# The first loads of an instance norm, split by even and odd partitions over two DMA queues

## The chip, the cores and the metric

The kernel runs on one core of one Trainium2 chip. The metric is the device time of one execution in microseconds (us), as the median of several runs.

## The reference

The input x has the shape 4 x 8 x 16 x 256 x 256 in float32 (134 MB). Each of its 4 x 8 x 16 = 512 channels, of 256 x 256 elements, is normalised by its own mean and variance and multiplied by a gamma per channel.

```python
def reference(x, gamma):
    mu = x.mean(axis=(3, 4), keepdims=True)
    var = ((x - mu) ** 2).mean(axis=(3, 4), keepdims=True)
    x_norm = (x - mu) / np.sqrt(var + 1e-5)
    out = x_norm * gamma[None, :, :, None, None]
    return out.astype(np.float32)
```

## The kernel before

The 512 channels are taken in 32 units of 16 channels. A channel is spread over 8 partitions, so a unit is one tile of 128 partitions x 8192 elements, 4 MiB, that lies in one piece in memory. Six such tiles, `slots`, hold the units in turn: unit u lies in `slots[u % 6]`.

The schedule is written out by hand, so each engine takes its instructions in the order of the code. Before the loop, two small transfers go out on the GpSimd queue: `touch` (8 KB, line 54) and the gamma row `g_row` (line 55). Then units 0 to 5 are loaded (line 48): units 1 and 3 on ScalarE's DMA queue, units 0, 2, 4 and 5 on SyncE's. GpSimd makes the averaging matrix `navg`, and VectorE (DVE) and TensorE (PE) spread gamma over the partitions: `g_rep` (line 81), `g_ps` (line 86) and `g_col` (line 92). These stand ahead of unit 0's work on DVE.

The loop then takes the units one by one. DVE sums the tile (line 105) while ScalarE (ACT) sums its squares (line 106). PE multiplies both sums with `navg` (line 114), which gives minus the mean and minus the mean square of each channel on all of its partitions. DVE, ACT and DVE turn these into the scale (lines 115, 119, 123, 125), and DVE applies mean and scale to the tile in place (line 128). The tile is stored on ScalarE's queue (line 132), and SyncE's queue loads unit u + 6 into the same slot, once that store has landed.

A transfer that is issued waits in its queue for those ahead of it; the two queues are served beside one another. The wait for a semaphore is done by the engine that issues (SyncE or ScalarE) and holds up what that engine would issue next.

Of the kernel before, what the change touches and what calls it, by code (L numbers as in the profile page):

```python
# [1 line left out]

# [4 lines left out]

F32 = mybir.dt.float32
U8 = mybir.dt.uint8
ALU = mybir.AluOpType  # L10
ACTF = mybir.ActivationFunctionType
AX = mybir.AxisListType


@with_exitstack
def kernel(
    ctx: ExitStack,
    tc: tile.TileContext,
    x: bass.AP,
    gamma: bass.AP,  # L20
    out: bass.AP,
):
    nc = tc.nc
    B, G, C, H, W = x.shape
    P = nc.NUM_PARTITIONS
    HW = H * W
    n_ch = B * G * C
    S = 8
    K = P // S
    F = HW // S  # L30
    U = n_ch // K
    NG = (G * C) // K
    AHEAD = 6
    assert HW % S == 0 and (G * C) % K == 0

    xv = x.rearrange("b g c h w -> (b g c h w)").rearrange("(u p f) -> u p f", p=P, f=F)
    ov = out.rearrange("b g c h w -> (b g c h w)").rearrange("(u p f) -> u p f", p=P, f=F)
    gv = gamma.rearrange("g c -> (g c)")

    data = ctx.enter_context(tc.tile_pool(name="data", bufs=1))  # L40
    singles = ctx.enter_context(tc.tile_pool(name="singles", bufs=1))
    psum = ctx.enter_context(tc.tile_pool(name="psum", bufs=4, space=bass.MemoryType.PSUM))
    ctx.enter_context(tc.manual_schedule())

    slots = [data.tile([P, F], F32, name=f"xt{i}") for i in range(AHEAD)]

    def load(u, queue):
        queue.dma_start(out=slots[u % AHEAD][:], in_=xv[u])  # L48


    g_row = singles.tile([1, G * C], F32, name="g_row")
    touch = singles.tile([16, 128], F32, name="touch")
    nc.vector.memset(touch[:], 0.0)  # L53
    nc.gpsimd.dma_start(out=ov[0][0::S, 0:128], in_=touch[:])  # L54
    nc.gpsimd.dma_start(out=g_row[:], in_=gv[None, :])  # L55
    for u in range(AHEAD):
        load(u, nc.scalar if u in (1, 3) else nc.sync)


    eps_t = singles.tile([P, 1], F32, name="eps_t")  # L60
    nc.gpsimd.memset(eps_t[:], 1e-5)
    one = singles.tile([1, 1], F32, name="one")
    nc.gpsimd.memset(one[:], 1.0)
    navg = singles.tile([P, K, S], F32, name="navg")
    nc.gpsimd.memset(navg[:], -1.0 / HW)  # L65
    nc.gpsimd.affine_select(  # L66
        out=navg[:], in_=navg[:], pattern=[[-S, K], [0, S]], compare_op=ALU.is_ge,
        fill=0.0, base=0, channel_multiplier=1,
    )
    nc.gpsimd.affine_select(  # L70
        out=navg[:], in_=navg[:], pattern=[[S, K], [0, S]], compare_op=ALU.is_ge,
        fill=0.0, base=S - 1, channel_multiplier=-1,
    )
    navg_w = navg[:].rearrange("p k s -> p (k s)")
    root_eps = singles.tile([P, 1], F32, name="root_eps")
    nc.scalar.activation(out=root_eps[:], in_=eps_t[:], func=ACTF.Sqrt)  # L76
    g_rep = singles.tile([1, NG, K, S], F32, name="g_rep")
    g_ps = psum.tile([P, NG], F32, name="g_ps", bufs=1)
    g_col = singles.tile([P, NG], F32, name="g_col")

    nc.vector.tensor_copy(  # L81
        out=g_rep[:],
        in_=g_row[:].rearrange("o (n k) -> o n k", n=NG).unsqueeze(3).to_broadcast([1, NG, K, S]),
    )
    for n in range(NG):
        nc.tensor.matmul(  # L86
            out=g_ps[:, n : n + 1],
            lhsT=g_rep[:, n].rearrange("o k s -> o (k s)"),
            rhs=one[:],
            start=True, stop=True,  # L90
        )
    nc.vector.tensor_copy(out=g_col[:], in_=g_ps[:])  # L92

    junk = singles.tile([P, F], U8, name="junk")

    st = singles.tile([P, U, 2], F32, name="st")
    nvar = singles.tile([P, U], F32, name="nvar")
    std = singles.tile([P, U], F32, name="std")
    rstd = singles.tile([P, U], F32, name="rstd")
    scale = singles.tile([P, U], F32, name="scale")  # L100

    squares = []
    for u in range(U):
        t = slots[u % AHEAD]
        nc.vector.reduce_sum(out=st[:, u, 0:1], in_=t[:], axis=AX.X)  # L105
        square = nc.scalar.activation(  # L106
            out=junk[:], in_=t[:], func=ACTF.Square, accum_out=st[:, u, 1:2],
        )
        if u:

            tc.declare_no_dep(square.ins, squares[-1].ins, reason="junk, ordered by the root between")
        squares.append(square)
        ps = psum.tile([P, 2], F32, name="ps")
        nc.tensor.matmul(out=ps[:], lhsT=navg_w, rhs=st[:, u], start=True, stop=True)  # L114
        nc.vector.tensor_scalar(  # L115
            out=nvar[:, u : u + 1], in0=ps[:, 0:1], scalar1=ps[:, 0:1],
            scalar2=ps[:, 1:2], op0=ALU.mult, op1=ALU.add,
        )
        nc.scalar.activation(  # L119
            out=std[:, u : u + 1], in_=nvar[:, u : u + 1], func=ACTF.Sqrt,  # L120
            bias=eps_t[:], scale=-1.0,
        )
        nc.vector.reciprocal(out=rstd[:, u : u + 1], in_=std[:, u : u + 1])  # L123
        g = u % NG
        nc.vector.tensor_mul(  # L125
            out=scale[:, u : u + 1], in0=rstd[:, u : u + 1], in1=g_col[:, g : g + 1],
        )
        nc.vector.tensor_scalar(  # L128
            out=t[:], in0=t[:], scalar1=ps[:, 0:1], scalar2=scale[:, u : u + 1],
            op0=ALU.add, op1=ALU.mult,  # L130
        )
        nc.scalar.dma_start(out=ov[u], in_=t[:])
        if u + AHEAD < U:
            load(u + AHEAD, nc.sync)


# [1 line left out]
_INS = ['x', 'gamma']  # L138
_OUTS = [((4, 8, 16, 256, 256), 'float32')]


# [23 lines left out]
```

## Time and profile before

| what | value |
|---|---|
| median of 3 runs | 626.87 us (626.68 to 627.37) |
| profiled execution, span from first to last instruction | 625.4 us (the page lists no other time of this execution) |
| DVE busy | 443.4 us (71%) |
| ACT busy | 238.8 us (38%) |
| PE busy | 21.4 us (3%) |
| moved by DMA | 268.46 MB, mean 429 GB/s |
| loads, issue to landing, median | 38.5 us on SyncE's queue, 31.7 us on ScalarE's |
| stores, issue to landing, median | 62.5 us |
| first reduction of unit 0 (line 105) starts | 22.57 us |
| first store issued | 37.63 us |
| last load issued and landed | 547.2 us, 585.7 us |
| last store issued | 600.8 us |

The page and the trace show one execution. Times of instructions count from the first one. A group's line gives its busy time and the mean time of one instruction, then the idle time of the engine before it and what ended that. The queue q1 is SyncE's, q10 is ScalarE's and q0 is GpSimd's. A window's last two columns are the mean busy share of the 16 DMA engines and what they moved in GB/s; a transfer's packets can put that share slightly over 1.

### The profile page before, as it was taken

What the parts mean: (1) busy time and instruction counts of PE and PEld (TensorE: products, weight loads), DVE (VectorE), ACT (ScalarE), POOL (GpSimd) and SP (SyncE); (2) the same over time, 40 slices, a digit from 0 to 9 for tenths busy, and PEclk for the clock granted to TensorE, in tenths of its full rate; (3) what the DMA queues carried; (4) which work ended last, traced back from release to release, by engine and by line L of the source; (5) the groups of instructions that cost most, each with busy time, mean ns of one, the idle gap of its engine ahead of it and who ended that gap; (6) DMA issues with size and microseconds to landing.
All of it is one profiled execution on the core that took longest, in us unless ns stands there. A gap on an engine that the chain in (4) does not pass through costs nothing.

```text
span 625.4 us, 631 instructions
## 1 busy us (share of the span) xinstructions
PE 21.4 (3%) x80; PEld 19.5 (3%) x80; DVE 443.4 (71%) x163; ACT 238.8 (38%) x98; POOL 2.4 (0%) x11
## 2 busy tenths in 40 slices
PE   0200000000000000000000000000000000000000
PEld 0200000000000000000000000000000000000000
DVE  0588999999776687666776767867668676686730
ACT  0444444444443244432344423444224442244400
POOL 1000000000000000000000000000000000000000
DMA  8999999999999999999999999999999999999998
GB/s 369 436 402 436 436 436 436 436 434 424 434 436 432 432 428 434 436 436 436 436 434 423 434 436 432 436 428 434 434 436 436 436 436 432 425 434 434 434 432 363
DMA packets 9282, 268.46 MB, mean 429 GB/s; under 512 B 1072, under 2 KB 1088, under 8 KB 1088
## 3 DMA queue, kind: packets, MB, share of 16 engines
q10 hardware_dynamic: 4896, 142.61, 52.9%
q1 hardware_dynamic: 4320, 125.83, 46.7%
q0 software_dynamic: 64, 0.01, 0.0%
q14 instruction: 2, 0.02, 0.0%
HBM read 134.22 MB, written 134.23 MB: 429 GB/s over the span
## 4 chain that ended last, share of the span: by engine, by line
another core or an unknown queue 61%; DMA 17%; DVE 15%; SPq 1%; PE 1%; issue 0%; ACT 0%
DVE st L105 10%; DMA xt<-in_x_dram 10%; DMA out_dram<-xt 8%; DVE xt L128 5%; SPq L48 1%; PE ps L114 1%; ACT std L119 0%; DVE nvar L115 0%; DVE rstd L123 0%; DVE scale L125 0%
## 5 line engine op out<-in xcount | busy, mean ns | idle before, releaser
L105 DVE TENSOR_REDUCE st<-xt 128x1 f32<-128x8192 f32 x32 | 277.9, 8685 | 100.8 <-DMA xt<-in_x_dram 100.8
L106 ACT ACTIVATE junk<-xt 128x8192 uint8<-128x8192 f32 x32 | 225.0, 7030 | 275.6 <-DMA xt<-in_x_dram 232.4
L128 DVE TENSOR_SCALAR xt<-xt,ps,scale 128x8192 f32<-128x8192 f32 x32 | 145.6, 4551 | 1.2
L119 ACT ACTIVATE std<-nvar,eps_t 128x1 f32<-128x1 f32 x32 | 9.4, 295 | 79.6 <-DVE nvar L115 79.6
L114 PE MATMUL ps<-st,navg 128*128 128x2 f32 x64 | 17.8, 348 | 557.6 <-DVE st L105 557.6
L114 PEld LDWEIGHTS ps<-st,navg 128*128 128x128 f32 x64 | 16.0, 311 | 559.4 <-issue 559.4
L115 DVE TENSOR_SCALAR nvar<-ps 128x1 f32<-128x1 f32 x32 | 9.2, 288 | 23.8 <-PE ps L114 23.8
L123 DVE RECIPROCAL rstd<-std 128x1 f32<-128x1 f32 x32 | 5.3, 164 | 11.6 <-ACT std L119 11.6
L81 DVE COPY g_rep<-g_row 1x1024 f32<-1x1024 f32 x1 | 0.7, 681 | 14.2 <-DMA g_row<-in_gamma_dram 14.2
L106 ACT ACTIVATION_READ_ACCUMULATOR junk<-xt 128x1 f32 x32 | 6.0, 187 | 0.0
L125 DVE TENSOR_TENSOR scale<-rstd,g_col 128x1 f32<-128x1 f32 x32 | 5.1, 160 | 1.1
L86 PE MATMUL g_ps<-one,g_rep 1*128 1x1 f32 x16 | 3.5, 347 | 16.1 <-DVE g_rep L81 16.1
L86 PEld LDWEIGHTS g_ps<-one,g_rep 1*128 1x128 f32 x16 | 3.5, 326 | 16.1 <-issue 16.1
L92 DVE COPY g_col<-g_ps 128x8 f32<-128x8 f32 x1 | 0.2, 167 | 3.7 <-PE g_ps L86 3.7
L76 ACT ACT_TABLE_LOAD x1 | 1.3, 1283 | 1.7 <-PEq L149 1.7
L53 DVE MEMSET touch<- 16x128 f32 x1 | 0.2, 165 | 0.9 <-PEq L149 0.9
L54 POOL DMA_DIRECT2D out_dram<-touch x1 | 0.6, 617 | 0.8 <-DVE touch L53 0.8
L55 POOL DMA_DIRECT2D g_row<-in_gamma_dram x1 | 0.5, 484 | 0.0
L66 POOL TENSOR_SCALAR_AFFINE_SELECT navg<-navg 128x128 f32<-128x128 f32 x1 | 0.4, 398 | 0.1
L70 POOL TENSOR_SCALAR_AFFINE_SELECT navg<-navg 128x128 f32<-128x128 f32 x1 | 0.4, 397 | 0.1
L65 POOL MEMSET navg<- 128x128 f32 x1 | 0.2, 231 | 0.0
L76 ACT ACTIVATE root_eps<-eps_t 128x1 f32<-128x1 f32 x1 | 0.2, 203 | 0.0
(6 smaller groups left out, 0.6 us busy)
## 6 DMA issues: line engine op xcount, KB each, us to landing
out_dram<-xt ACTq DMA_DIRECT2D x32, 4096.0 KB, 62.5
xt<-in_x_dram SPq DMA_DIRECT2D x30, 4096.0 KB, 38.5
xt<-in_x_dram ACTq DMA_DIRECT2D x2, 4096.0 KB, 31.7
out_dram<-touch POOLq DMA_DIRECT2D x1, 8.0 KB, 9.1
g_row<-in_gamma_dram POOLq DMA_DIRECT2D x1, 0.5 KB, 13.3
```

The lines of the kernel that those rows point to most:

```text
L48: queue.dma_start(out=slots[u % AHEAD][:], in_=xv[u])
L76: nc.scalar.activation(out=root_eps[:], in_=eps_t[:], func=ACTF.Sqrt)
L81: nc.vector.tensor_copy(out=g_rep[:], in_=g_row[:].rearrange("o (n k) -> o n k", n=NG).unsqueeze(3).to_broadcast([1, NG, K, S]),)
L86: nc.tensor.matmul(out=g_ps[:, n : n + 1], lhsT=g_rep[:, n].rearrange("o k s -> o (k s)"), rhs=one[:], start=True, stop=True,)
L105: nc.vector.reduce_sum(out=st[:, u, 0:1], in_=t[:], axis=AX.X)
L106: square = nc.scalar.activation(out=junk[:], in_=t[:], func=ACTF.Square, accum_out=st[:, u, 1:2],)
L114: nc.tensor.matmul(out=ps[:], lhsT=navg_w, rhs=st[:, u], start=True, stop=True)
L115: nc.vector.tensor_scalar(out=nvar[:, u : u + 1], in0=ps[:, 0:1], scalar1=ps[:, 0:1], scalar2=ps[:, 1:2], op0=ALU.mult, op1=ALU.add,)
L119: nc.scalar.activation(out=std[:, u : u + 1], in_=nvar[:, u : u + 1], func=ACTF.Sqrt, bias=eps_t[:], scale=-1.0,)
L123: nc.vector.reciprocal(out=rstd[:, u : u + 1], in_=std[:, u : u + 1])
L125: nc.vector.tensor_mul(out=scale[:, u : u + 1], in0=rstd[:, u : u + 1], in1=g_col[:, g : g + 1],)
L128: nc.vector.tensor_scalar(out=t[:], in0=t[:], scalar1=ps[:, 0:1], scalar2=scale[:, u : u + 1], op0=ALU.add, op1=ALU.mult,)
```

## The change

Units 0 to 3 are loaded one after the other, each in two halves: SyncE's queue loads the even partitions (64 partitions with a step of 2), ScalarE's the odd ones. Unit 0 is stored in the same two halves, on both queues. The loads of units 4 and 5 are moved from ahead of the loop to behind unit 0's store, on SyncE's queue. All other stores and loads stay as they were.

```diff
     def load(u, queue):
         queue.dma_start(out=slots[u % AHEAD][:], in_=xv[u])
 
+    SHARED = 4
+
+    def halves(u):
+        return [(queue, slots[u % AHEAD][h::2, :], xs) for queue, h, xs in
+                ((nc.sync, 0, slice(0, P, 2)), (nc.scalar, 1, slice(1, P, 2)))]
+
...
-    for u in range(AHEAD):
-        load(u, nc.scalar if u in (1, 3) else nc.sync)
+    for u in range(SHARED):
+        for queue, rows, xs in halves(u):
+            queue.dma_start(out=rows, in_=xv[u][xs])
...
-        nc.scalar.dma_start(out=ov[u], in_=t[:])
+        if u == 0:
+            for queue, rows, xs in halves(u):
+                queue.dma_start(out=ov[u][xs], in_=rows)
+            for v in range(SHARED, AHEAD):
+                load(v, nc.sync)
+        else:
+            nc.scalar.dma_start(out=ov[u], in_=t[:])
         if u + AHEAD < U:
             load(u + AHEAD, nc.sync)
```

In the changed kernel SyncE's order is thus: four half loads, half of store 0, loads 4 and 5, then load 6 and on. ScalarE's is: four half loads, its work on unit 0, half of store 0, its work on unit 1, store 1, and on.

## The prediction

> **What bounds the kernel now.** I read the DMA part of the page first, because the kernel reads 134 MB and writes 134 MB and computes little.
>
> ```profile
> DMA packets 9282, 268.46 MB, mean 429 GB/s; under 512 B 1072, under 2 KB 1088, under 8 KB 1088
> ## 3 DMA queue, kind: packets, MB, share of 16 engines
> q10 hardware_dynamic: 4896, 142.61, 52.9%
> q1 hardware_dynamic: 4320, 125.83, 46.7%
> ```
>
> The two hardware queues' packets take 52.9 + 46.7 = 99.6% of what 16 DMA engines have in the span of 625.4 us. That is 622.9 us of transfer and 2.5 us in which an engine waits, start and last receipt included. No compute engine comes near: DVE is busy 443.4 us. The chain of waits says the same, in repeated steps:
>
> ```profile
> 179.79 18.95 another core or an unknown queue
> 198.74 0.02 SPq L48
> 198.77 0.03 issue
> 198.80 0.33 SPq L48
> 199.12 18.97 another core or an unknown queue
> ```
>
> One turn is 198.77 - 179.43 = 19.35 us, in which one unit is loaded and one stored: 9.67 us for a transfer of 128 x 8192. 64 of them are 619 us. The windows view, last two columns DMA share and GB/s, shows that no part of the run is left open:
>
> ```profile
> 20.00:40.00 20.00, 0.56 (x2) 0.50 (x2) 16.25 (x6) 9.39 (x4) 0.00 (x0) 1.00 0.98 421
> 40.00:60.00 20.00, 0.56 (x2) 0.50 (x2) 18.82 (x6) 12.48 (x5) 0.00 (x0) 1.00 1.01 418
> 100.00:560.00 460.00, 13.94 (x50) 12.53 (x50) 341.15 (x125) 183.19 (x75) 0.00 (x0) 1.00 1.00 433
> 600.00:620.00 20.00, 0.00 (x0) 0.00 (x0) 0.76 (x1) 0.00 (x0) 0.00 (x0) 1.00 1.02 442
> ```
>
> Loads alone (20 to 40 us), loads beside stores (100 to 560) and stores alone on one queue (600 to 620) all run at a share near 1.00. So the end is set by the bytes and by how well 16 engines move them. Starting unit 0 earlier cannot bring more than a part of the 2.5 us; a form of transfer that goes slower costs its whole excess.
>
> **The change, part by part.** The working is against the span of 625.4 us. The median of the three runs, 626.87, lies 1.47 us above it, and I carry that over. Of the profiled execution the page gives no time but its span.
>
> *Loads 0 to 3.* Four transfers of 128 rows become eight of 64 rows, four on each queue. Bytes and row length (8192 elements) stay. Four more issues cost 0.33 to 0.60 us each (the issue rows of SP and ACT), beside queued transfers: only ACT's two added issues stand ahead of its table load (1.28 us), and ACT has nothing to do until 22.57. That is zero on the path; without that cover it would be under 1.2 us.
>
> No row shows a transfer of 64 partitions, so its price is bounded. By bytes, a half is 9.67 / 2 = 4.84 us: eight halves are 38.7 us, as now, change 0. By transfer, as if half the partitions took as long as all (the one form that the trace prices), a half is 9.67 us: eight are 77.4 us, change +38.7. A gain is excluded beyond the idle 2.5 us. Between the ends I take the upper one. The rate of 9.67 us is shown only for transfers that run over all 128 partitions, where two such transfers beside one another share it without loss. A half takes every second partition, so whatever split of rows gave each of the 16 engines its own part of a full tile need not hold for it.
>
> [...]
>
> *Store 0.* It becomes two halves and waits for the same DVE result. By bytes +0, by transfer +9.7. Here I take the middle, +4.8: one store goes alone with no load beside it, and stores alone are the best window of the table (442 GB/s).
>
> *What starts earlier.* Load 0 by bytes lands at 0.81 + 2.40 + 9.67 = 12.9 us; 2.40 is what the first pair took beyond two transfers (21.74 - 19.34). DVE cannot use all of it: its copy of g_col ends at 19.87, after the gamma transfer landed at 15.29. So the first reduction starts at 19.9 instead of 22.57, and store 0 is issued at 37.63 - 2.70 = 34.9. The value of these 2.7 us is zero, since the queues are then full of loads until 41.9. With halves at the upper price load 0 lands at 22.6 and nothing is earlier at all.
>
> *The new wait.* On SP, store 0's half waits for DVE's last step of unit 0, and loads 4 and 5 are queued behind it; they were issued at once before. At 34.9 this is 7.0 us ahead of 41.9, when loads 0 to 3 land, so the engines still have work, and I count zero. If that cover went, each us of delay past it would be a us at the end.
>
> *The order after it.* Load 4 now runs beside store 1, so load u beside store u - 3 instead of u - 4. The number of transfers is the same: four loads alone, then one store alone, 28 pairs, three stores alone instead of four. Load 31 lands one transfer later (595.4 instead of 585.7), its store is issued at 600.80 + 9.67 = 610.5, while store 30 runs until 625.4 - 9.67 = 615.7. The slack falls from 14.9 to 5.2 us and still covers the issue. Zero, and without that cover up to the shortfall.
>
> Sum: 38.7 + 4.8 = +43.5 us; 626.87 + 43.5 = 670.4.
>
> **The rivals.**
>
> *Nothing moves (not slower).* The mechanism: 64 strided rows spread over the 16 engines as cleanly as 128 do, so a half costs 4.84 us. Place: the first 50 us. Price: the same number of rows is moved, so 626.9, give or take 1.0. The dip of the second and third windows (421 and 418 against 433, 20 us each, (12 + 15) / 433 x 20 = 1.2 us) is all that could be regained or doubled. For it: all three mixtures of queues and directions above run at the same share. Against it: none of these has a partition stride. It decides from the point at which a shared load's rate is above nine tenths of 433 GB/s.
>
> [...]
>
> *The wait on SP binds.* Store 0 comes after the loads have drained: the price is its delay past 41.9, for example 5 us if the gamma transfer landed 12 us later than 15.29 (19.87 + 12 = 31.9, store 0 at 46.9): 632. Against it: gamma has the same two queues beside it as now.
>
> *Faster.* The start's and the dip's losses vanish: at most 2.5 + 1.2 us; 625.0 is as far as I would go. The 99.6% speaks against more.
>
> **How the numbers follow.** Halves near the upper price (650 to 676): 0.47. Part of the excess (629 to 650): 0.11. SP's wait: 0.03. Nothing moves, within 0.2% (1.25 us, about what a measurement of this kernel can tell from no change): 0.33. Faster by more than that: 0.06. So slower 0.61, same 0.33, faster 0.06. The likeliest is 670.4, its own range 650 to 676. Since two cases of quite different size hold most of the chance, the range reaches from the lower part of the unmoved case, 626.0, to both prices in full, 626.87 + 48.4 = 675.3.
>
> **What would show it.** In the profile after, at the forecast: slices 1 to 5 show about half the GB/s, 210 to 260, with the DMA share still near 1; loads 0 and 1 land around 22 and 41 us, load 3 near 80; the turns of the chain further on are 19.35 us as before, shifted. If load 1 lands at about 22.6 and load 3 at 42, and the early slices read above 400 GB/s, halves cost by bytes and the time is unmoved. If slices 1 to 3 are full and a later one empty, it is SP's wait. If the tail shows DMA share below 1 before the last store, the slack of 5.2 us was too small. A turn other than 19.35 us beyond 120 us would mean that the change reaches further than unit 0 to 4, which I have no price for.

## The result and the profile after

The changed kernel took 645.21 us (median of 4 runs, 644.54 to 646.16) against 627.10 us of the kernel before on the same chip. The ratio is 1.0291, 95% interval 1.0278 to 1.0304: slower by 18.1 us. The forecast was slower by 43.5 us, at another place.

The profiled execution took 646.16 us with a span of 644.0 us. The DMA part of its page:

```profile
DMA packets 9362, 268.47 MB, mean 417 GB/s; under 512 B 1152, under 2 KB 1168, under 8 KB 1168
## 3 DMA queue, kind: packets, MB, share of 16 engines
q10 hardware_dynamic: 4864, 140.51, 50.8%
q1 hardware_dynamic: 4432, 127.93, 47.7%
```

The bytes are the same, but the packets themselves take longer: 50.8 + 47.7 = 98.5% of 644.0 us is 634.3 us of transfer on the mean engine, where it was 622.9. That is 11.4 of the 18.6 us by which the spans differ. The other 7.2 us are time in which the mean engine has nothing to move (9.7 us, where it was 2.5). The windows view (last two columns DMA share and GB/s) says where:

```profile
20.00:40.00 20.00, 0.56 (x2) 0.50 (x2) 18.82 (x6) 8.42 (x4) 0.00 (x0) 1.00 1.01 433
100.00:200.00 100.00, 2.79 (x10) 2.50 (x10) 70.37 (x26) 37.17 (x16) 0.00 (x0) 1.00 1.00 424
400.00:500.00 100.00, 2.80 (x10) 2.51 (x10) 68.63 (x25) 37.08 (x15) 0.00 (x0) 1.00 1.00 423
...
616.00:620.00 4.00, 0.00 (x0) 0.00 (x0) 4.00 (x1) 3.76 (x2) 0.00 (x0) 1.00 0.91 393
620.00:624.00 4.00, 0.56 (x2) 0.50 (x2) 2.82 (x5) 0.29 (x1) 0.00 (x0) 1.00 0.68 295
624.00:628.00 4.00, 0.00 (x0) 0.00 (x0) 3.67 (x1) 0.00 (x0) 0.00 (x0) 1.00 0.47 205
```

The half loads run at 433 GB/s from 20 to 40 us, where the whole loads before had 421: they cost nothing extra there. The longer packets lie in the long mixed stretch, whose transfers the change leaves whole: 423 to 424 GB/s at a full share, where the kernel before had 433. Then, at the end, engines run dry one after the other (a share of 0.91, 0.68 and 0.47 from 616 to 628 us), since the last store is issued only at 627.70.

The timeline view gives the price of a unit. These are reductions of units 6 and 31, each waiting for its load (start, duration, operation, idle before and what ended it):

```profile
111.25 8.69 DVE L112 TENSOR_REDUCE st<-xt 128x1 f32<-128x8192 f32 x1 [3.77 <-DMA xt<-in_x_dram]
...
612.64 8.69 DVE L112 TENSOR_REDUCE st<-xt 128x1 f32<-128x8192 f32 x1 [5.04 <-DMA xt<-in_x_dram]
```

They are (612.64 - 111.25) / 25 = 20.06 us apart. In the kernel before, unit 31 was at

```profile
585.74 8.69 DVE L105 TENSOR_REDUCE st<-xt 128x1 f32<-128x8192 f32 x1 [4.33 <-DMA xt<-in_x_dram]
```

and unit 10 at 179.25 us (the line stands below): (585.74 - 179.25) / 21 = 19.36 us. The difference is 0.70 us a unit, 17.4 us in 25 units. From the last reduction's start to the end of the span it is 31.4 us; before it was 39.7 us with one store more in the queue, 39.7 - 9.7 = 30.0, so the end adds 1.4 us. Together that is 18.8 us, for spans that differ by 18.6.

This is more than the 11.4 us that the mean engine lost, and the packet records of the trace say why. Each of the 16 engines writes its own end of a transfer to a semaphore, and the reductions that wait for a load start 0.35 to 0.50 us behind the last of the 16 writes (units 9 to 31 before, 6 to 31 after). In the changed kernel the 16 ends of load 4 come within 0.5 us; those of load 31 come between 598.9 and 612.3 us, 13.3 us apart, and the spread grows all the way. In the kernel before they are never more than 1.1 us apart. So the pace of 20.06 us is that of the slowest engine, and the faster ones have nothing left at the end.

What is different in that stretch is seen by setting two lines of the timeline beside one another: a reduction starts when its load has landed, and SyncE issues its next load when the store beside it has landed (0.34 to 0.71 us behind the store's last semaphore write, in both kernels). In the kernel before:

```profile
179.25 8.69 DVE L105 TENSOR_REDUCE st<-xt 128x1 f32<-128x8192 f32 x1 [4.33 <-DMA xt<-in_x_dram]
179.46 19.66 SPq L48 DMA_DIRECT2D xt<-in_x_dram  x2
```

In the changed kernel:

```profile
171.46 8.69 DVE L112 TENSOR_REDUCE st<-xt 128x1 f32<-128x8192 f32 x1 [4.58 <-DMA xt<-in_x_dram]
174.05 40.34 SPq L48 DMA_DIRECT2D xt<-in_x_dram  x3
```

Before, a load and the store beside it land together (0.21 us between the lines). After, the store lands 2.6 us behind the load, and so on for the whole run (3.3 us at 552 us). I call this gap the lag. The packet records explain its size: a packet is one row of 8192 elements (32 KB, 1.21 us in the median), and a transfer of 128 rows is eight packets on each of 16 engines and then a semaphore write. The records of an engine (each put to the engine whose last record ends where it starts) alternate between its two queues, semaphore writes included: from 100 to 560 us, 6830 of 6832 steps from one record to the next change the queue in the kernel before, and 6633 of 6663 in the changed one. At the end of a load (L), beside a store (S), with the semaphore writes starred, the records of an engine read:

```
before:  L S L S L* S* L S L S
after:   L S L S L* S L S* L S
```

So the store is one packet behind, and one packet of each queue is 2 x 1.21 = 2.4 us. The lag stems from the first microseconds. ScalarE's first packet came 1.76 us after SyncE's before, behind one packet on each engine, and 3.08 us after it in the changed kernel, behind two. From then on both queues had work (the steps between queues above), and the gap stayed open: 2.6 us at 171 us, 3.3 us at 552 us. From 60 us after the first packet on, 634 packets take over 1.24 us (22 before). 511 of them are load packets, and 421 of these stand at most three records behind a semaphore write; the excess of the 634 is 11 us on the mean engine.

### The profile page after: what moved, and what is told of

Same layout as the page of the kernel before. It is cut to its first block, busy times and chain, and to the rows that moved or that the text cites. A ratio compares the mean times of both kernels' runs of the same rounds, so it can differ in the third digit from the quotient of the medians.

```text
span 644.0 us, 644 instructions
## 1 busy us (share of the span) xinstructions
PE 21.4 (3%) x80; PEld 19.5 (3%) x80; DVE 443.5 (69%) x163; ACT 238.8 (37%) x98; POOL 2.4 (0%) x11
## 3 DMA queue, kind: packets, MB, share of 16 engines
q10 hardware_dynamic: 4864, 140.51, 50.8%
q1 hardware_dynamic: 4432, 127.93, 47.7%
## 4 chain that ended last, share of the span: by engine, by line
DVE 67%; another core or an unknown queue 20%; issue 4%; PE 3%; DMA 2%; ACT 2%; POOL 0%
DVE st L112 43%; DVE xt L135 21%; PE ps L121 3%; DMA g_row<-in_gamma_dram 2%; ACT std L126 2%; DVE nvar L122 1%; DVE rstd L130 1%; DVE scale L132 1%; PE g_ps L93 1%; DVE g_rep L88 0%; POOL out_dram L60 0%; DVE touch L59 0%; DVE g_col L99 0%
## 6 DMA issues: line engine op xcount, KB each, us to landing
g_row<-in_gamma_dram POOLq DMA_DIRECT2D x1, 0.5 KB, 11.3
```

## The experiments

Each of the runs below is compared with the kernel before on its own chip (626.85 to 627.02 us).

**One part at a time.** The first run halves the loads alone: loads 4 and 5 stay ahead of the loop, store 0 is whole.

```diff
     for u in range(SHARED):
         for queue, rows, xs in halves(u):
             queue.dma_start(out=rows, in_=xv[u][xs])
+    for u in range(SHARED, AHEAD):
+        load(u, nc.sync)
...
-        if u == 0:
...
+        nc.scalar.dma_start(out=ov[u], in_=t[:])
```

> Only the first part of the change: units 0 to 3 load in halves, while loads 4 and 5 stay ahead of the loop and store 0 is one whole transfer on ScalarE's queue, so load u runs beside store u - 4 as before. Theory A (lag: in the changed kernel ScalarE's first packet came two SyncE packets late instead of one, and from then on the two queues end their transfers one packet apart): the lag is there, so about 645 us. Theory B (pairing: load u beside store u - 3 is what slows the packets): about 627 us. Theory C (half loads leave the 16 engines uneven): about 645 us.

Measured: 644.26 us, ratio 1.0275 (1.026 to 1.029). The second run does the other part alone, with whole loads 0 to 3:

```diff
     for u in range(SHARED):
-        for queue, rows, xs in halves(u):
-            queue.dma_start(out=rows, in_=xv[u][xs])
+        load(u, nc.scalar if u in (1, 3) else nc.sync)
```

> Only the second part: whole loads 0 to 3 as before on alternating queues, but store 0 in halves ahead of load 4, loads 4 and 5 behind it, so load u runs beside store u - 3. Theory A (lag): the first packets alternate as before, so about 627 us. Theory B (pairing): about 645 us. Theory C (half loads): about 627 us.

Measured: 627.72 us, ratio 1.0011 (1.0001 to 1.002). So load u beside store u - 3 is not what is slow (theory B falls), and nearly the whole 18 us come with the half loads. This run did not land its transfers together either, though I had expected it to: its timeline shows a lag of 7.3 us, three packets.

```profile
166.15 8.69 DVE L111 TENSOR_REDUCE st<-xt 128x1 f32<-128x8192 f32 x1 [5.09 <-DMA xt<-in_x_dram]
173.41 39.07 SPq L48 DMA_DIRECT2D xt<-in_x_dram  x3
```

**The lag or the halves.** The third run keeps every half transfer and holds back SyncE's first load.

```diff
+    nc.vector.memset(slots[0][0:1, 0:1536], 0.0)
     for u in range(SHARED):
```

> The changed kernel with SyncE's first half load held back by some 1 us (it waits for a memset of one row of its tile on VectorE), so that the first packets of both queues can alternate. Theory A (lag): about 627 us, slow packets gone. Theory B (pairing) and C (half loads): about 645 us.

Measured: 628.11 us, ratio 1.0019 (1.001 to 1.0029). The half transfers are all there and the loss is gone (theory C falls). The memset overshot: now the store lands 3.0 us ahead of the load.

```profile
168.58 38.98 SPq L48 DMA_DIRECT2D xt<-in_x_dram  x3
171.61 8.69 DVE L113 TENSOR_REDUCE st<-xt 128x1 f32<-128x8192 f32 x1 [4.35 <-DMA xt<-in_x_dram]
```

The fourth run puts a lag into the kernel before:

```diff
+    nc.vector.memset(slots[1][0:1, 0:1536], 0.0)
     for u in range(AHEAD):
         load(u, nc.scalar if u in (1, 3) else nc.sync)
```

> The kernel before with ScalarE's first load held back by some 1 us in the same way (a memset of one row of unit 1's tile), so that SyncE's queue is two packets ahead instead of one. Theory A (lag): about 645 us, with slow load packets from about 80 us on. Theory B (pairing) and C (half loads): about 627 us.

Measured: 627.00 us, ratio 1.0002 (0.9992 to 1.0011), with a lag of 6.3 us on its timeline, three packets in the records. Theory A as I had put it, that any lag is slow, is wrong. What was left of it was a lag of one packet, store behind load (theory A2). Two shorter memsets, 64 and 768 elements, were to give one and two packets.

> The kernel before with ScalarE's first load held back by about 0.6 us (a memset of 64 elements of one row of unit 1's tile), a third of the delay of the run with 1536 elements, whose stores then ended three packets behind the loads beside them. Theory A2 (only a lag of one packet, the store behind the load, is slow; whole or half loads make no difference): about 644 us. Theory C2 (the half loads are needed besides the lag): about 627 us. If the first packets still alternate, about 627 us and nothing is learnt.

> The same with a memset of 768 elements, which should give a lag of two packets. Theory A2 (one packet alone is slow): about 627 us. A variant of it, that the loss falls with the lag from one to three: between 628 and 640 us.

Measured: 626.84 us (ratio 0.9998, 0.9989 to 1.0007) and 627.07 us (1.0002, 0.9993 to 1.0012). The timelines show lags of 4.8 and 6.0 us (two packets, and two to three, in the records), so neither hit one packet, and both are as fast as before. ScalarE's issue moved by only 0.35 us in the first of them (1.16 against 0.81 us) and the lag by 4.6 us, two packets: the start could not be set finely in this way. What was left was to add a record to one of the alternating queues. A transfer cut in two has one more semaphore write on each engine: the kernel before with store 14 cut (the last run below) has 16 packets more on ScalarE's queue, 4912 for 4896, each under 512 B.

```diff
+        if u == 0:
+            for h in range(2):
+                nc.scalar.dma_start(out=ov[u][h::2, :], in_=t[h::2, :])
+        else:
             nc.scalar.dma_start(out=ov[u], in_=t[:])
```

> The kernel before with one edit: store 0 goes out as two half transfers, both on ScalarE's queue. The extra transfer ends with one more semaphore write, which takes one more turn of that queue, so from then on stores should end one packet (2.4 us) behind the loads beside them, with whole loads throughout and load u beside store u - 4. Theory A2 (a lag of one packet is slow by itself): about 644 us. Theory C2 (half loads are needed too): about 627 us.

Measured: 643.76 us, ratio 1.0269 (1.0254 to 1.0283). One store of the kernel before, cut in two, costs 17 us: all loads are whole. Its windows and timeline read like those of the changed kernel, with 422 to 424 GB/s and a lag that began at one packet in the records and reads 3.5 us here:

```profile
400.00:500.00 100.00, 2.78 (x10) 2.50 (x10) 69.22 (x25) 37.09 (x15) 0.00 (x0) 1.00 1.00 423
```

```profile
181.20 8.69 DVE L105 TENSOR_REDUCE st<-xt 128x1 f32<-128x8192 f32 x1 [4.62 <-DMA xt<-in_x_dram]
184.70 19.73 SPq L48 DMA_DIRECT2D xt<-in_x_dram  x2
```

The reverse takes the lag out of the changed kernel by one more half transfer, now on SyncE's queue:

```diff
-            for v in range(SHARED, AHEAD):
-                load(v, nc.sync)
+            for _, rows, xs in halves(SHARED):
+                nc.sync.dma_start(out=rows, in_=xv[SHARED][xs])
+            load(SHARED + 1, nc.sync)
```

> The changed kernel with one edit: load 4 goes out as two half transfers, both on SyncE's queue, which gives that queue one more semaphore write and takes the lag away from load 5 on. Theory A2 (lag): about 627 us, though one more transfer is halved. Theory C2 (half transfers leave something behind): about 645 us or more.

Measured: 628.13 us, ratio 1.0019 (1.0004 to 1.0033). With twelve half transfers instead of ten, the kernel is 17 us faster than the changed one; load and store land 0.2 us apart again and the rate is back.

```profile
400.00:500.00 100.00, 2.79 (x10) 2.50 (x10) 69.91 (x26) 37.77 (x16) 0.00 (x0) 1.00 1.00 432
```

```profile
169.92 8.69 DVE L112 TENSOR_REDUCE st<-xt 128x1 f32<-128x8192 f32 x1 [4.33 <-DMA xt<-in_x_dram]
170.14 39.41 SPq L48 DMA_DIRECT2D xt<-in_x_dram  x3
```

The third test of theory A2 has no half transfer at all: the late ScalarE of the run with 1536 elements, and a tiny load on SyncE's queue that was to take two turns there.

```diff
+    tiny = singles.tile([16, 128], F32, name="tiny")
+    nc.vector.memset(slots[1][0:1, 0:1536], 0.0)
     for u in range(AHEAD):
         load(u, nc.scalar if u in (1, 3) else nc.sync)
+        if u == 4:
+            nc.sync.dma_start(out=tiny[:], in_=xv[0][0:16, 0:128])
```

> The kernel before with ScalarE's first load late as in the run with 1536 elements (stores three packets behind, 627 us), and a tiny extra load of 16 x 128 elements on SyncE's queue behind load 4, which takes two turns of that queue and so leaves a lag of one packet, with no half transfer anywhere. Theory A2: about 644 us. Theory C2: about 627 us.

Measured: 643.1, 665.1, 667.5 and 668.3 us. All four lose, and one by what theory A2 expected, but three lost over twice that. The packet records of the profiled one (665.1 us) show that it is not the test I had meant: from load 6 on, 14 of the 16 engines have the lag of one packet, and two end load and store together. On these two ScalarE's first packet had come one packet earlier (6.41 and 6.56 us, the others 7.40 to 7.82). And it is these two that fall behind: from load 6 to load 13 the slowest engine, one of them, takes 20.8 us a load, the others 19.6 to 20.1. They end each load last, so the timeline reads hardly any lag:

```profile
184.91 8.69 DVE L109 TENSOR_REDUCE st<-xt 128x1 f32<-128x8192 f32 x1 [6.29 <-DMA xt<-in_x_dram]
185.14 21.65 SPq L48 DMA_DIRECT2D xt<-in_x_dram  x2
```

So ends that meet are not fast in themselves: beside engines with a lag of one packet, the engines without it were the slow ones. A theory of a fixed price per unit, paid by each engine for its own lag, does not give that, and the size of this loss stays unexplained.

**Why this lag.** Three edits of the changed kernel tried what could stall a packet there. One issues load u + 6 three units later in the code:

```diff
+    LATE = 3
+    gate = singles.tile([1, 1], F32, name="gate")
...
-        if u + AHEAD < U:
-            load(u + AHEAD, nc.sync)
+        w = u - LATE
+        if w >= 0 and w + AHEAD < U:
+            nc.vector.tensor_copy(out=gate[:], in_=slots[w % AHEAD][0:1, 0:1])
+            load(w + AHEAD, nc.sync)
```

> The changed kernel, lag and all, but load u + 6 is issued three units later in the code, behind VectorE's work on unit u + 3 (a copy of one element of the slot makes it wait), so that SyncE no longer issues a load about 2 to 3 us after a load has landed. Theory D (the issue of a load, its descriptors coming in beside running load packets just then, stalls them): about 627 us. Theory F (the stall lies in the transfers themselves, ends of loads and stores one packet apart): about 645 us.

Measured: 645.23 us, ratio 1.0293 (1.0277 to 1.0308), with SyncE's issue moved from 2.6 to 15.1 us behind the start of a reduction. The issue of a load just behind a landing is not the cause. One takes ScalarE's square over 8 elements:

```diff
-            out=junk[:], in_=t[:], func=ACTF.Square, accum_out=st[:, u, 1:2],
+            out=junk[:, 0:8], in_=t[:, 0:8], func=ACTF.Square, accum_out=st[:, u, 1:2],
```

> The changed kernel with ScalarE's square taken over 8 of the 8192 elements (the variance is left out in effect, the rest of the work stays), so that ScalarE hardly reads the tile. Theory E (the reads of a landed tile by ScalarE beside VectorE hold up the load packets that follow a landing): clearly below 645 us. Theories D and F: about 645 us.

Measured: 644.59 us, ratio 1.0282 (1.0258 to 1.0306). ScalarE's reads are not the cause. One moves all stores by 1 MiB in memory:

```diff
+    orow = out.rearrange("b g c h w -> (b g c h w)").rearrange("(r f) -> r f", f=F)
+    SHIFT = 32
...
-                queue.dma_start(out=ov[u][xs], in_=rows)
+                queue.dma_start(out=orow[SHIFT + xs.start:SHIFT + P:2], in_=rows)
...
-            nc.scalar.dma_start(out=ov[u], in_=t[:])
+            if u < U - 1:
+                nc.scalar.dma_start(out=orow[u * P + SHIFT:(u + 1) * P + SHIFT], in_=t[:])
+            else:
+                nc.scalar.dma_start(out=orow[u * P + SHIFT:], in_=t[0:P - SHIFT])
+                nc.scalar.dma_start(out=orow[0:SHIFT], in_=t[P - SHIFT:])
```

> The changed kernel with each store moved by 32 rows (1 MiB) in the output, so the lag of one packet stays but the addresses that loads and stores touch at the same time are others (the last store is cut in two to fit; the output is shifted). Theory G (what is slow is a set of addresses in memory that meet only at that lag): well below 645 us, near 627. Theory F (the order of transfer ends on the DMA engines is what is slow): about 645 us.

Measured: 649.28 us, ratio 1.0359 (1.0342 to 1.0376). Still slow, with a lag of 2.9 us, so addresses that meet at one exact distance are not the cause; other distances were not tried. The 4 us more include a last store in two parts and were not taken apart.

**Once or at each unit.** Two runs change the lag in the middle, by a cut transfer as above: load 16 of the changed kernel, store 14 of the kernel before.

```diff
-        if u + AHEAD < U:
+        if u + AHEAD == 16:
+            for _, rows, xs in halves(16):
+                nc.sync.dma_start(out=rows, in_=xv[16][xs])
+        elif u + AHEAD < U:
```

> The changed kernel with load 16 in two half transfers on SyncE's queue, which takes the lag of one packet away from load 17 on. If the loss is paid anew at each unit under the lag (theory A2) and the engines fall back into step when it is gone: 11 to 12 of the 27 slow units stay, so about 627 + 18 x 0.42 = 634 to 636 us. If the engines, once out of step, stay slow: about 645 us.

> The kernel before with store 14 in two half transfers on ScalarE's queue, which brings the lag of one packet in for the pairs from store 15 on (13 of 28). Theory A2 with a price per unit: 627 + 17 x 13 / 27 = about 635 us, the first half of the run as fast as before. If the lag only hurts where it stands from the start of the run: about 627 us.

Measured: 645.81 us (ratio 1.0296, 1.0279 to 1.0313) and 635.06 us (1.0129, 1.0114 to 1.0144). The second is as theory A2 had it: 433 to 435 GB/s up to 300 us, 422 from 400 to 500, and half the loss. So the loss is paid unit by unit from where the lag comes in. The first missed theory A2's 634 to 636 us and came out at the 645 us of the other alternative, engines that stay slow. It does not decide between them, since the edit did more than move one turn. The tile of unit 12 was ready at 245.9 us, but its store was issued only at 270.7, when load 14 had landed; ScalarE's queue had run almost empty by then (2 or 3 packets started in 2.4 us, where 16 is usual). Behind that the engines end their loads and stores one to four packets apart, and the timeline, which shows the slowest engine, still has a gap of 3.2 us:

```profile
432.51 8.69 DVE L112 TENSOR_REDUCE st<-xt 128x1 f32<-128x8192 f32 x1 [4.82 <-DMA xt<-in_x_dram]
435.67 20.43 SPq L48 DMA_DIRECT2D xt<-in_x_dram  x2
```

**What is shown and what is open.** The lags and times together:

| run | store lands behind its load (us) | time (us) |
|---|---|---|
| third (all halves, SyncE late) | -3.0 | 628.11 |
| kernel before | 0.2 | 627.10 |
| load 4 in two | 0.2 | 628.13 |
| half loads alone | 2.4 | 644.26 |
| square over 8 elements | 2.4 | 644.59 |
| changed kernel | 2.6 | 645.21 |
| stores moved by 1 MiB | 2.9 | 649.28 |
| store 0 in two | 3.5 | 643.76 |
| memset of 64 | 4.8 | 626.84 |
| memset of 768 | 6.0 | 627.07 |
| memset of 1536 | 6.3 | 627.00 |
| store 0 in halves, whole loads | 7.3 | 627.72 |
| late ScalarE and tiny load | 0.2 (one packet on 14 engines, none on two) | 643.1 to 668.3 |

Shown is that in these runs, where all engines stood alike, packets were slow when a store ended one packet behind the load beside it, with and without half transfers (643.76 to 649.28 us), and not when it ended one packet ahead, with the load, or two and three packets behind (626.84 to 628.13 us). The last row of the table limits this: there the slowest engines had no lag of their own. Why one packet behind is special is open: the issue of loads just behind a landing, ScalarE's reads, the pairing of units and addresses at one exact distance are excluded. Not tried was a change of the semaphore writes themselves, of VectorE's reads of a landed tile, or loads and stores with their queues exchanged.

No version here is faster than the kernel before.

## Why the prediction was right and wrong

The sign was right by luck: the term that it rested on came to nothing, and a term put at zero made the kernel slower. The amount of 43.5 us was nearly two and a half times the 18.1 us that were measured.

*The price of a half load* is the step that failed: I took the upper of two bounds, 38.7 us, as if 64 rows cost as much as 128. The window from 20 to 40 us reads 433 GB/s, and ScalarE's square of unit 0 starts at 14.51 us, where it started at 22.57: the lower bound, 0, was right. My ground was that no row showed a strided half; the row of 421 GB/s for loads alone was the nearer one, since it held the same packets (32 KB, 1.21 us in both kernels). No run shows a half at 9.67 us, the term behind the 38.7 us: in the changed kernel SyncE's four halves end at 11.73, 21.42, 31.11 and 40.94 us, so a pair of halves takes 9.7 us and a half the 4.84 us that it has by bytes.

*Store 0*, put at 4.8 us, cost hardly anything: cut the same way with whole loads ahead, the kernel came to 627.72 us, 0.7 above the kernel before.

*What starts earlier and the wait on SP* were as worked out, each at zero: the first reduction starts at 17.79 us (19.9 predicted, gamma landed 2 us sooner, 11.3 us from its issue for 13.3), store 0 is issued at 32.84, and loads 4 and 5 wait behind it with the queues full.

*The slack of the tail*, 5.2 us, had been called enough, with a DMA share below 1 ahead of the last store as the sign that it was not. The sign came (0.47 from 624 to 628 us): the last load lands when its slowest engine is done, and the faster ones are through with store 30 by then. Its price, 1.4 us, belongs to the lag; with the lag taken away (load 4 in two, the same order of units) the share is 1.02 from 616 to 620 us.

*The turn of 19.35 us* is where the time went; it stood in the sum unchanged, which is the second step that failed. The prediction named a turn other than this beyond 120 us as a thing it had no price for. It came to 20.06 us over 25 units, 17.4 us in all. I had noticed 99.6% busy engines and taken from this that a packet's duration is a constant; the fully busy DMA share of 1.00 after the change, at 423 GB/s, shows that it is not. The step that would have caught it is to ask, of every edit to a queue, not only how much it carries but in which order the ends of its transfers now meet those of the other queue.

*The rivals:* "nothing moves" was right on the first 50 us and wrong on the rest. The case of part of the excess (629 to 650 us, 0.11) has the measured 645.21 us in its range, by luck: that excess was to come from the half loads, and they lost nothing. None of the rivals had the mechanism.

## What to carry to other kernels

In this kernel, whose DMA engines are 99.6% busy, one packet more at the start (two ahead of ScalarE's first, for one) moved the distance between two queues for the whole run. On another kernel of this kind, look at the distance between a load's and a store's landing in the steady stretch, before and after (0.2 and 2.6 us here). If it has moved, a transfer cut in two on one queue is worth a try: with load 4 in two, the distance came back to 0.2 us and the kernel within 1.2 us of the kernel before. Look at the other transfers too: with load 16 in two, a store went out 24.8 us late. And look at the spread of the engines' ends (13.3 us at load 31 here), since a reduction waited for the last of the 16. A full DMA share said that the engines had work, not at what rate they moved it: read GB/s beside it (a share of 1.00 at 433 GB/s before and at 423 after).

## What the runs showed of the hardware

- In the changed kernel the two queues kept their distance for hundreds of us: a lag set in the first 6 us (ScalarE's first packet 3.08 us behind SyncE's) read 2.6 us at 171 us and 3.3 us at 552 us.
- The records of an engine alternate between the two queues, and the semaphore write at the end of a transfer stands among them in a place of its own (L S L S L* S L S* in the changed kernel; 6633 of 6663 steps from 100 to 560 us change the queue). Cutting store 0 in two moved the lag from 0.2 to 3.5 us and the time by 16.8 us.
- One lag of the five tried (one packet ahead, none, one, two and three behind), that of one packet behind, went with 0.70 us more a unit (20.06 against 19.36 us); the runs with the others lie at most 1.2 us above the kernel before.
- Under that lag, in the changed kernel, the 16 engines drifted apart: 0.5 us at the end of load 4, 13.3 us at the end of load 31 (before: at most 1.1 us).
- Loads of every second partition, on two queues at once, moved at 433 GB/s from 20 to 40 us, where whole loads had 421; a pair of halves took 9.7 us, and a whole load 9.67 us.
